# An eighth Strassen pair in the down projections, with their casts tied in order

## The chip, the cores and the metric

The kernel runs on one core of one Trainium2 chip. The metric is the device time of one execution in microseconds (us); lower is better. Three executions of the kernel before took 2194.71, 2195.12 and 2196.28 us, with the median 2195.12.

## The reference, cut to what matters

The program is one layer of a streaming encoder on 256 tokens of width 2048: a SwiGLU feed-forward block (FFN), gated token mixers, cross-attention, and a second FFN, each between two RMSNorms. The change touches the two FFNs alone:

```python
def swiglu(h, w_gate, w_up, w_down):
    return (jax.nn.silu(h @ w_gate) * (h @ w_up)) @ w_down
...
    h = rmsnorm(x, n_ffn1_pre[l])
    x = x + 0.5 * rmsnorm(swiglu(h, w_ffn1_gate[l], w_ffn1_up[l], w_ffn1_down[l]), n_ffn1_post[l])
```

`w_gate` and `w_up` are 2048 x 5504, `w_down` is 5504 x 2048, all f32. The down projection therefore sums over 5504 = 43 x 128 hidden units, that is over 43 k-tiles, which the kernel numbers k = 0 to 42.

## The kernel before

**Three matmuls for one.** The weights are f32. Each tile of weights `raw` is cut into a high part (`hi`, ScalarE cast to fp32r) and the rest (`lo = raw - hi`, VectorE subtraction). The activations are cut the same way, for the down projection into `mh` and `ml`. One product is then three TensorE matmuls: `mh*hi`, `mh*lo` and `ml*hi` (`product`, lines 544 to 546, in the wide part; lines 460 to 462 in `lin_tok_steps`, the narrow part).

**The down projection.** The 2048 output columns are done in two halves, b = 0 and b = 1, of 1024 columns; each half has two narrow columns, c = 2b and c = 2b + 1, of 512. The tokens are two groups t of 128. So a half has four accumulators `own[t][h]`, each one PSUM bank of 128 x 512. With four more banks (`shared`, called p1, p5, p7 and p6) all eight banks are in use.

**The wide part** (`lin_wide`) takes k = 0 to 29 with weight tiles of 128 x 1024. An ordinary k-tile takes 2 x 2 products, 12 matmuls, into `own`. The k-tiles 4 to 17 are taken as seven pairs (`SPAIRS`), with the Strassen-Winograd scheme: a pair would take eight products, and takes seven (21 matmuls). The sums of weights that this needs are four VectorE additions (lines 570 to 573) on the two raw tiles `ra` and `rb`, in place, after their own parts are cut. The sums of activations are made earlier, where gate and up end, by `left` (lines 510 to 513), and are kept in the tile `S`. Three products of a pair go straight to `own`, four to `shared`.

**Order.** `_wide_order` lists three ordinary k-tiles, then each pair followed by two ordinary ones. TensorE follows this order by hand (`manual_schedule`). On the other engines a list scheduler orders the instructions by priority when the program is built; `ahead(self.lead)` gives casts, splits and additions of weights a priority 100 steps earlier. `after(ins, prev)` adds an edge that fixes the order of two instructions. `cut` does a cast and a split; its outputs go round a ring of six slots, three of `whi`/`wlo` and three of `room`. In the first pair the cuts are, in order of the program: three ordinary tiles, the first half of `ra`, `rb`; then, after the additions, `ra` again and `rb` again; then the next two ordinary tiles. The first five are tied in this order by `after`, the later ones are not. The loads go round four `wraw` buffers and the two halves of a tile `raws`.

**After the wide part** comes `narrow(c + 1, 30 to 35)`, which continues the odd column's banks; then `fix_wide` adds the shared products onto the four banks of `own` (one ScalarE copy, line 594, and eight VectorE additions, lines 595 to 602, in a buffer `part` of the pool `wraw`); then `narrow(c, 30 to 42)` continues the even column's banks, `own[0][0]` and `own[1][0]`, and so waits for what `fix_wide` adds to them; then `narrow(c + 1, 36 to 42)`. In `narrow` one weight tile holds two k-tiles of 512 columns, and takes 2 x 2 x 3 = 12 matmuls. Its casts and splits are lines 365 and 366.

In the second half, `done` and `refill` start four loads of the residual X from POOL, two during the last pairs and two in `narrow(c + 1)`, because X has the memory that the first part of `S` had.

Of the kernel before, what the change touches and what calls it, by code (L numbers as in the profile page):

```python
# [10 lines left out]
F32 = mybir.dt.float32  # L11
# [7 lines left out]
P = 128  # L19
# [7 lines left out]
WT = 1024  # L27
# [6 lines left out]
LEAD = 100  # L34
FIRST = 1000000
TOK_US, CH_US = 0.65, 0.33
SPAIRS = range(2, 9)
WIDE, EARLY = 30, 36


def _wide_order():
# [184 lines left out]
class Layer:  # L226
# [275 lines left out]
            for t in range(NT):  # L502
                evac(t, ps[t])

    def left(self, g0, g1, mh, ml, k, sh, sl):


        nc = self.nc
        d = self.tmp.tile([P, 512], F32, tag="junk", name="sums").rearrange("p (a t) -> p a t", a=4)
        nc.vector.tensor_sub(d[:, 0], g0[:, P:], g1[:, P:])  # L510
        nc.vector.tensor_sub(d[:, 1], d[:, 0], g0[:, :P])
        nc.vector.tensor_sub(d[:, 2], g0[:, :P], g0[:, P:])
        nc.vector.tensor_add(d[:, 3], g1[:, :P], d[:, 1])
        self.split(g1, mh[:, k + 1, :], ml[:, k + 1, :])
        self.split(d[:, 0], mh[:, k, P:], ml[:, k, P:])
        self.split(d[:, 1:], sh, sl)

    def lin_wide(self, w, b, mh, ml, sums, ring, raws, banks, done):

        nc = self.nc
        own, shared = banks
        seen, turn = set(), [0]
        last = _wide_order()[-1]

        def cut(raw):
            n = raw.shape[-1]
            hi, lo = (x[:, :n] for x in ring[turn[0] % len(ring)])
            turn[0] += 1  # L530
            before = self.last_cast, self.last_split
            with self.ahead(self.lead):
                self.last_cast = nc.scalar.copy(out=hi, in_=raw)  # L533
                self.last_split = nc.vector.tensor_sub(out=lo, in0=raw, in1=hi.bitcast(F32))  # L534
            if turn[0] < 6:
                for ins, prev in zip((self.last_cast, self.last_split), before):
                    self.after(ins, prev)
            return [(self.paired(hi[:, i : i + 512]), self.paired(lo[:, i : i + 512])) for i in range(0, n, 512)]

        def product(bank, x, wt, stop=False):  # L540
            (xh, xl), (hi, lo) = x, wt
            start = id(bank) not in seen
            seen.add(id(bank))
            nc.tensor.matmul(bank, xh, hi, start=start, stop=False)  # L544
            nc.tensor.matmul(bank, xh, lo, start=False, stop=False)  # L545
            nc.tensor.matmul(bank, xl, hi, start=False, stop=stop)  # L546

        def load():
            i = self.wide_at % 6
            raw = raws[:, i - 4] if i > 3 else self.wraw.tile([P, WT], F32, tag="wraw", name="wraw")  # L550
            o = P * WT * (b * KF + self.wide_at)
            nc.sync.dma_start(out=raw, in_=w[o : o + P * WT].rearrange("(p x) -> p x", p=P))
            self.wide_at += 1
            return raw

        at = lambda k, t: tuple(x[:, k, t * P : (t + 1) * P] for x in (mh, ml))
        self.wide_at = 0
        for item in _wide_order():
            if isinstance(item, int):
                halves = cut(load())  # L560
                for t in range(NT):
                    for h in range(2):
                        product(own[t][h], at(item, t), halves[h], item == last)
                continue
            k0, k1 = item
            ra, rb = load(), load()
            a0, a1, b0, b1 = ra[:, :512], ra[:, 512:], rb[:, :512], rb[:, 512:]
            (w11,), (w21, w22) = cut(a0), cut(rb)
            with self.ahead(self.lead):
                nc.vector.tensor_add(a0, a0, a1)  # L570
                nc.vector.tensor_add(a1, a1, b1)  # L571
                nc.vector.tensor_add(b1, a0, b1)
                nc.vector.tensor_add(b0, b1, b0)
            (e1, e3), (e4, e2) = cut(ra), cut(rb)
            s2, s3, s4 = sums(k0 // 2 - SPAIRS[0])
            end = k0 // 2 == SPAIRS[-1]
            product(shared[0], at(k0, 0), w11, end)
            product(own[0][0], at(k1, 0), w21)
            product(own[0][1], s4, w22)
            product(shared[1], at(k0, 1), e1, end)  # L580
            product(shared[2], s3, e3, end)
            product(shared[3], s2, e2, end)
            product(own[1][0], at(k1, 1), e4)
            done(k0 // 2 - SPAIRS[0])
        self.cuts = turn[0]

    def fix_wide(self, banks, part):


        nc = self.nc  # L590
        own, (p1, p5, p7, p6) = banks
        u, v = part[:, :512], part[:, 512:]
        add, sub = nc.vector.tensor_add, nc.vector.tensor_sub
        self.after(nc.scalar.copy(out=u, in_=p1), self.last_cast)
        self.after(add(own[0][0], own[0][0], u), self.last_split)
        add(u, p6, u)
        sub(v, p5, u)
        add(u, p7, u)
        add(own[1][0], own[1][0], u)
        add(own[0][1], own[0][1], v)  # L600
        sub(v, v, p7)
        add(own[1][1], own[1][1], v)

    def rstd(self, ss, n, half=False, weight=1.0):

# [192 lines left out]
    def ffn(self, normed, wg, wu, wd, post, residual, *after):  # L798
# [3 lines left out]
        with self.tc.tile_pool(name="hid", bufs=1) as hid:  # L802
# [3 lines left out]
                 self.hpool.tile([P, 8, 2, P], F32R, tag="yh", bufs=2, name="S"))  # L806

            def sums(n):
                x, n = (S[0], n) if n < 5 else (S[1], n - 5)
                return x[:, 3 * n : 3 * n + 3]  # L810

            def evacs(c0):
                gate = {}

                def ev_gate(j, ps):
                    sg = hid.tile([P, T], F32, tag="sg", name="sg", bufs=2)
                    nc.vector.tensor_mul(sg, ps, row())
                    nc.scalar.activation(out=sg, in_=sg, func=AF.Silu)
                    nc.vector.tensor_mul(sg, sg, row())
                    gate[j] = sg  # L820

                def ev_up(j, ps):
                    k = c0 // P + j
                    nc.vector.tensor_mul(gate[j], ps, gate[j])
                    if k // 2 not in SPAIRS:
                        self.split(gate[j], mh[:, k, :], ml[:, k, :])
                    elif j == 0:
                        self.split(gate[j][:, :P], mh[:, k, :P], ml[:, k, :P])
                    else:
                        v = sums(k // 2 - SPAIRS[0])  # L830
                        self.left(gate[0], gate[1], mh, ml, k - 1, v[:, :, 0], v[:, :, 1])

                return ev_gate, ev_up

# [45 lines left out]
            def refill():  # L880
                i = fresh.pop()
                t, s = i // 2, slice(i % 2 * 1024, (i % 2 + 1) * 1024)
                self.after(nc.gpsimd.dma_start(
                    out=self.X[:, t, s], in_=residual[t * P : (t + 1) * P, s]), self.last_split)
# [11 lines left out]
            def lin(c, ev, passage):  # L896
                b = c // 2
                if c % 2:
                    narrow(c, range(EARLY, KF, 2), ev, (7 if passage else SKEW) * (c == 3), passage)
                    return  # L900
                make = lambda pool, tag: [pool.tile([P, 512], F32, tag=tag, name="mm") for _ in range(2)]
                one = [make(self.pst, "tr"), make(self.pss, "sm")]
                two = [make(self.psm, "mm"), make(self.psm, "mm")]
                own, shared = (two, one) if b else (one, two)
                banks[b] = [list(x) for x in zip(*own)], [x for p in shared for x in p]
                with self.tc.manual_schedule(engines={mybir.EngineType.PE}):
                    if b:
                        self.X = self.hpool.tile([P, NT, D], F32, tag="big", bufs=1, name="X")
                        fresh.extend((3, 2, 1, 0))
                    order = slots[self.turn :] + slots[: self.turn]  # L910
                    self.lin_wide(wd, b, mh, ml, lambda n: [(x[:, 0], x[:, 1]) for x in (sums(n)[:, i] for i in range(3))],
                                  order + more, raws, banks[b], lambda n: n > 4 and fresh and refill())
                    self.turn = (self.turn + self.cuts % (2 * RING)) % RING if self.cuts % (2 * RING) < RING else self.turn
                    narrow(c + 1, range(WIDE, EARLY, 2), None, 0, None)
                    self.fix_wide(banks[b], self.wraw.tile([P, WT], F32, tag="wraw", name="part"))
                    narrow(c, range(WIDE, KF, 2), ev, 0, None)

            return self.post_norm(lin, post, True, *after)
# [1024 lines left out]
```

## Time and profile before

| What | Value |
|---|---|
| median of three executions | 2195.12 us (2194.71 to 2196.28) |
| profiled execution | 2195.21 us |
| span from first to last instruction | 2193.4 us |
| TensorE (PE) busy, matmul | 2161.4 us, 99% |
| weight loads (PEld) | 1926.9 us, 88% |
| VectorE (DVE) | 1617.8 us, 74% |
| ScalarE (ACT) | 1190.3 us, 54% |
| HBM read | 438.61 MB |

The rows of the profile name an engine, a line of the kernel, the operation, the tiles written and read, and times in us (`xN` is a count; ns where said). "Idle before" an instruction is the time in which its engine waited, with the engine that ended the wait. A matmul's row is longer than the time until the next matmul may start, because matmuls overlap: TensorE's pace is read from starts.

### The profile page before, as it was taken

How to read it: one execution, taken by the hardware profiler on the slowest of the kernel's cores; microseconds unless marked ns; L12 is line 12 of the kernel's file. 1: busy time of each engine (PE TensorE's matmuls, PEld its weight loads, DVE VectorE, ACT ScalarE, POOL GpSimd, SP SyncE). 2: the span in 40 equal slices, each digit the busy share in tenths (PEclk: the TensorE clock that was granted, in tenths of full speed). 3: DMA queues.
4: the chain of work that ended last, by engine and by line, in shares of the span. 5: the costliest groups of instructions: out<-in, count | busy, mean ns of one | idle time of the engine just before them, and what ended most of it. 6: DMA issues, size and time to landing. Idle time of an engine off the chain costs nothing.

```text
span 2193.4 us, 35347 instructions
## 1 busy us (share of the span) xinstructions
PE 2161.4 (99%) x13580; PEld 1926.9 (88%) x13580; DVE 1617.8 (74%) x2402; ACT 1190.3 (54%) x1794; POOL 110.5 (5%) x185
## 2 busy tenths in 40 slices
PE   9999999999999999999999999999999999999998
PEld 8999999988888888988777889988999999998886
DVE  7777666688887677768778766657777766679696
ACT  7555555555556565664444556446555555555553
POOL 0000000000000000101342000000000000000000
PEclk9999999999999999999999999999999999999999
DMA  7666666665766664555867765546666666666665
GB/s 251 203 201 202 202 201 202 201 232 203 228 219 227 220 204 150 186 172 184 253 200 243 274 212 192 176 164 219 198 202 201 201 201 202 201 221 223 200 233 170
DMA packets 132361, 453.51 MB, mean 207 GB/s; under 512 B 16352, under 2 KB 17888, under 8 KB 131936
## 3 DMA queue, kind: packets, MB, share of 16 engines
q1 hardware_dynamic: 123408, 429.84, 59.4%
q0 software_dynamic: 7920, 20.98, 3.1%
q8 instruction: 106, 1.74, 0.3%
q10 hardware_dynamic: 864, 0.44, 0.1%
q14 instruction: 63, 0.52, 0.1%
HBM read 438.61 MB, written 12.59 MB: 206 GB/s over the span
## 4 chain that ended last, share of the span: by engine, by line
PE 45%; DVE 5%; issue 1%; DMA 1%; ACT 1%; POOL 0%; DVEq 0%; POOLq 0%; ACTq 0%
PE mm L421 16%; PE mm L425 8%; PE mm L460 5%; PE mm L462 4%; PE mm L461 4%; PE mm L545 2%; PE mm L546 2%; PE mm L544 2%; DVE wlo L366 2%; ACT whi L365 0%; DVE tm L1415 0%; DVE TT L1418 0%; PE xo L1817 0%; PE tr L663 0%; DMA raws<-in_w_ffn_down 0%
## 5 line engine op out<-in xcount | busy, mean ns | idle before, releaser
L366 DVE TENSOR_TENSOR wlo<-wraw,whi 128x1024 fp32r<-128x1024 f32 (+3 forms) x672 | 806.3, 1202 | 422.8 <-ACT whi L365 414.2
L421 PE MATMUL mm<-hT,whi 128*128 128x512 f32 x3280 | 1078.6, 384 | 0.7 <-DVE hT L654 0.7
L365 ACT CAST whi<-wraw 128x1024 fp32r<-128x1024 f32 (+3 forms) x672 | 692.0, 1031 | 580.8 <-PE mm L462 207.6
L425 PE MATMUL mm<-hT,wlo 128*128 128x256 f32 x3280 | 880.0, 274 | 0.6 <-DVE wlo L366 0.6
L421 PEld LDWEIGHTS mm<-hT,whi 128*128 128x128 f32 x3280 | 614.1, 190 | 81.7 <-ACT whi L365 1.2
L425 PEld LDWEIGHTS mm<-hT,wlo 128*128 128x128 f32 x3280 | 630.1, 192 | 6.7 <-DVE wlo L366 1.0
L461 PE MATMUL mm<-wlo,hT 128*128 128x512 f32 (+2 forms) x512 | 180.0, 352 | 4.0 <-DVE wlo L366 3.8
L460 PE MATMUL mm<-whi,hT 128*128 128x512 f32 (+2 forms) x512 | 182.5, 356 | 0.9 <-DVE gt L1602 0.7
L462 PE MATMUL mm<-whi,hT 128*128 128x512 f32 (+2 forms) x512 | 178.3, 349 | 0.3 <-DVE hT L654 0.3
L433 ACT COPY half<-mm 128x256 f32<-128x256 f32 x206 | 75.5, 368 | 115.6 <-PE mm L421 115.6
L434 DVE TENSOR_TENSOR half<-half,mm 128x256 f32<-128x256 f32 x206 | 85.7, 417 | 40.4 <-ACT half L433 40.4
L461 PEld LDWEIGHTS mm<-wlo,hT 128*128 128x128 f32 x512 | 97.1, 190 | 18.3 <-DVE wlo L366 9.5
L460 PEld LDWEIGHTS mm<-whi,hT 128*128 128x128 f32 x512 | 97.1, 190 | 12.6 <-DVE gt L1602 1.1
L544 PE MATMUL mm<-whi,mh 128*128 128x512 f32 x284 | 107.6, 379 | 0.0
L545 PE MATMUL mm<-wlo,mh 128*128 128x512 f32 x284 | 107.6, 379 | 0.0
L546 PE MATMUL mm<-whi,ml 128*128 128x512 f32 x284 | 107.6, 379 | 0.0
L462 PEld LDWEIGHTS mm<-whi,hT 128*128 128x128 f32 x512 | 97.1, 190 | 10.0 <-DVE hT L654 1.2
L534 DVE TENSOR_TENSOR wlo<-wraw,whi 128x1024 fp32r<-128x1024 f32 x60 | 72.0, 1222 | 18.3 <-ACT whi L533 17.7
L533 ACT CAST whi<-wraw 128x1024 fp32r<-128x1024 f32 x60 | 61.3, 1048 | 31.6 <-ACT whi L533 9.0
L533 ACT CAST room<-wraw 128x1024 fp32r<-128x1024 f32 (+1 forms) x56 | 49.6, 893 | 51.3 <-DVE wraw L571 46.4
L460 PE MATMUL mm<-whi,mh 128*128 128x512 f32 x200 | 75.8, 379 | 0.0
L461 PE MATMUL mm<-wlo,mh 128*128 128x512 f32 x200 | 75.8, 379 | 0.0
(373 smaller groups left out, 2787.8 us busy)
## 6 DMA issues: line engine op xcount, KB each, us to landing
wraw<-in_w_ffn_up SPq DMA_DIRECT2D x171, 512.0 KB, 4.3
wraw<-in_w_ffn_gate SPq DMA_DIRECT2D x170, 512.0 KB, 4.3
wraw<-in_w_ffn_down SPq DMA_DIRECT2D x128, 512.0 KB, 4.6
wraw<-in_w_in SPq DMA_DIRECT2D x124, 512.0 KB, 3.8
raws<-in_w_ffn_down SPq DMA_DIRECT2D x40, 512.0 KB, 4.9
wraw<-in_w_o SPq DMA_DIRECT2D x32, 512.0 KB, 4.3
wraw<-in_w_ckv SPq DMA_DIRECT2D x32, 512.0 KB, 4.1
wraw<-in_w_oa SPq DMA_DIRECT2D x16, 512.0 KB, 3.6
```

Source lines behind the costliest of these rows:

```text
L365: cast = self.last_cast = nc.scalar.copy(out=hi[:, e], in_=raw[:, e])
L366: self.last_split = nc.vector.tensor_sub(out=lo[:, e], in0=raw[:, e], in1=hi[:, e].bitcast(F32))
L421: both = lambda: nc.tensor.matmul(ps[j], hi[:, s], self.woven(x[:, k]), start=(k == 0), stop=(k == nk - 1))
L425: nc.tensor.matmul(ps[j][:, 0, :], lo[:, s], self.woven(x[:, k, 0]), start=False, stop=False)
L434: nc.vector.tensor_add(tokens, tokens, high)
L460: nc.tensor.matmul(ps[t], part(xh, t, k), hi, start=(k == first and not begun), stop=False, **more)
L461: nc.tensor.matmul(ps[t], part(xh, t, k), lo, start=False, stop=False, **more)
L462: self.last_mm = nc.tensor.matmul(ps[t], part(xl, t, k), hi, start=False, stop=(k == last), **more)
L533: self.last_cast = nc.scalar.copy(out=hi, in_=raw)
L544: nc.tensor.matmul(bank, xh, hi, start=start, stop=False)
L545: nc.tensor.matmul(bank, xh, lo, start=False, stop=False)
L546: nc.tensor.matmul(bank, xl, hi, start=False, stop=stop)
```

## The change

`SPAIRS` gets an eighth pair, k = 18 and 19, and the wide part grows from k < 30 to k < 34, so that each pair still has two ordinary k-tiles behind it. `narrow(c + 1)` before `fix_wide` shrinks from k = 30 to 35 to k = 34 and 35, and `narrow(c)` starts at 34. All cuts of the wide part are tied in order, not the first five alone. `fix_wide` works in `raws`, which the wide part no longer needs then, in place of a buffer of `wraw`; its additions start with `p6 + u`, and are tied one after another. The sums of activations of the first pair (n = 0) lie in what was left free in `S`, one block in its first tile and two in its second, so that `left` splits them in two instructions. The refill of X starts one pair later, with the two last pairs as before.

```diff
-SPAIRS = range(2, 9)
-WIDE, EARLY = 30, 36
+SPAIRS = range(2, 10)
+WIDE, EARLY = 34, 36
...
-    def left(self, g0, g1, mh, ml, k, sh, sl):
+    def left(self, g0, g1, mh, ml, k, places):
...
-        self.split(d[:, 1:], sh, sl)
+        i = 1
+        for x in places:
+            n = x.shape[1]
+            self.split(d[:, i : i + n], x[:, :, 0], x[:, :, 1])
+            i += n
...
-            if turn[0] < 6:
-                for ins, prev in zip((self.last_cast, self.last_split), before):
-                    self.after(ins, prev)
+            for ins, prev in zip((self.last_cast, self.last_split), before):
+                self.after(ins, prev)
...
-        u, v = part[:, :512], part[:, 512:]
+        (u, x), (v, z) = [(part[:, i, :512], part[:, i, 512:]) for i in range(2)]
         add, sub = nc.vector.tensor_add, nc.vector.tensor_sub
         self.after(nc.scalar.copy(out=u, in_=p1), self.last_cast)
-        self.after(add(own[0][0], own[0][0], u), self.last_split)
-        add(u, p6, u)
-        sub(v, p5, u)
-        add(u, p7, u)
-        add(own[1][0], own[1][0], u)
-        add(own[0][1], own[0][1], v)
-        sub(v, v, p7)
-        add(own[1][1], own[1][1], v)
+        prev = self.last_split
+        for f, *args in ((add, x, p6, u), (sub, v, p5, x), (add, x, p7, x), (add, own[0][0], own[0][0], u),
+                         (add, own[1][0], own[1][0], x), (sub, z, v, p7), (add, own[0][1], own[0][1], v),
+                         (add, own[1][1], own[1][1], z)):
+            ins = f(*args)
+            self.after(ins, prev)
+            prev = ins
...
             def sums(n):
-                x, n = (S[0], n) if n < 5 else (S[1], n - 5)
-                return x[:, 3 * n : 3 * n + 3]
+                if n == 0:
+                    return S[0][:, 15:], S[1][:, 6:]
+                x, n = (S[0], n - 1) if n < 6 else (S[1], n - 6)
+                return (x[:, 3 * n : 3 * n + 3],)
...
-                                  order + more, raws, banks[b], lambda n: n > 4 and fresh and refill())
+                    self.lin_wide(wd, b, mh, ml, parts, order + more, raws, banks[b],
+                                  lambda n: n > 5 and fresh and refill())
...
                     narrow(c + 1, range(WIDE, EARLY, 2), None, 0, None)
-                    self.fix_wide(banks[b], self.wraw.tile([P, WT], F32, tag="wraw", name="part"))
+                    self.fix_wide(banks[b], raws)
                     narrow(c, range(WIDE, KF, 2), ev, 0, None)
```

More of the change, by code (lines that the diff above doesn't have):

```diff
@@ L808, in sums, with parts @@
             def sums(n):
-                x, n = (S[0], n) if n < 5 else (S[1], n - 5)
-                return x[:, 3 * n : 3 * n + 3]
+                if n == 0:
+                    return S[0][:, 15:], S[1][:, 6:]
+                x, n = (S[0], n - 1) if n < 6 else (S[1], n - 6)
+                return (x[:, 3 * n : 3 * n + 3],)
+            def parts(n):
+                return [(x[:, i, 0], x[:, i, 1]) for x in sums(n) for i in range(x.shape[1])]
             def evacs(c0):
@@ L829, in ev_up @@
                     else:
-                        v = sums(k // 2 - SPAIRS[0])
-                        self.left(gate[0], gate[1], mh, ml, k - 1, v[:, :, 0], v[:, :, 1])
+                        self.left(gate[0], gate[1], mh, ml, k - 1, sums(k // 2 - SPAIRS[0]))
                 return ev_gate, ev_up
@@ L910, in lin @@
                     order = slots[self.turn :] + slots[: self.turn]
-                    self.lin_wide(wd, b, mh, ml, lambda n: [(x[:, 0], x[:, 1]) for x in (sums(n)[:, i] for i in range(3))],
-                                  order + more, raws, banks[b], lambda n: n > 4 and fresh and refill())
+                    self.lin_wide(wd, b, mh, ml, parts, order + more, raws, banks[b],
+                                  lambda n: n > 5 and fresh and refill())
                     self.turn = (self.turn + self.cuts % (2 * RING)) % RING if self.cuts % (2 * RING) < RING else self.turn
                     narrow(c + 1, range(WIDE, EARLY, 2), None, 0, None)
-                    self.fix_wide(banks[b], self.wraw.tile([P, WT], F32, tag="wraw", name="part"))
+                    self.fix_wide(banks[b], raws)
                     narrow(c, range(WIDE, KF, 2), ev, 0, None)
```

## The prediction

> **What bounds the kernel now.** I read the page first, then the busy time of two windows, the waits of TensorE, and last the instructions in order of time around the start and the end of the wide part. From the page:
>
> ```profile
> span 2193.4 us, 35347 instructions
> PE 2161.4 (99%) x13580; PEld 1926.9 (88%) x13580; DVE 1617.8 (74%) x2402; ACT 1190.3 (54%) x1794; POOL 110.5 (5%) x185
> L544 PE MATMUL mm<-whi,mh 128*128 128x512 f32 x284 | 107.6, 379 | 0.0
> ```
>
> TensorE is the bound, so the change is worth the matmuls it takes away and the time in which TensorE waits. For the price of a matmul the 379 ns of its row won't do, as rows overlap. The first matmul of the narrow part behind the wide one, and the one 36 matmuls later (k = 30 to 35, six each):
>
> ```profile
> 534.33 0.38 PE L460 MATMUL mm<-whi,mh 128*128 128x512 f32 x1
> 542.10 0.38 PE L460 MATMUL mm<-whi,mh 128*128 128x512 f32 x1
> ```
>
> 7.77 us for 36 matmuls is 0.216 us each. That is the price here.
>
> The windows (length, then busy time of PE, PEld, DVE, ACT and POOL, each with its count, clock, DMA share, GB/s), one in the gate and up stage, one in the middle of a wide part:
>
> ```profile
> 60.00:440.00 380.00, 380.00 (x2323) 349.43 (x2322) 270.93 (x405) 201.18 (x305) 0.00 (x0) 1.00 0.62 201
> 480.00:527.00 47.00, 47.00 (x220) 41.15 (x219) 44.62 (x51) 27.18 (x29) 0.00 (x0) 1.00 0.64 217
> ```
>
> In both TensorE has no gap. But in the wide part VectorE is at 44.62 of 47.00, 95%, against 71% in gate and up: the wide part has little room on VectorE, and a late start there shows. It does, in the waits of TensorE:
>
> ```profile
> PE mm L545 <- DVE wlo L534: 3.5, 4, 1.0
> ```
>
> Four waits, one in each wide part (two FFNs, two halves), for a split of the wide part. The row counts from the modelled end of the matmul before, so the loss is read from starts. These are the matmuls, in order, around each such wait: first and third matmul of the product e1 of the first pair (line 544 `room,mh`, 546 `room,ml`), then of its product e2 (`whi,S`); in the first wide part e1 has no gap.
>
> ```profile
> 470.86 0.38 PE L544 MATMUL mm<-whi,S 128*128 128x512 f32 x1
> 472.60 0.38 PE L546 MATMUL mm<-whi,S 128*128 128x512 f32 x1
> ...
> 577.71 0.38 PE L544 MATMUL mm<-room,mh 128*128 128x512 f32 x1
> 578.45 0.38 PE L546 MATMUL mm<-room,ml 128*128 128x512 f32 x1
> 579.32 0.38 PE L544 MATMUL mm<-whi,S 128*128 128x512 f32 x1
> 580.73 0.38 PE L546 MATMUL mm<-whi,S 128*128 128x512 f32 x1
> ...
> 1975.29 0.38 PE L544 MATMUL mm<-room,mh 128*128 128x512 f32 x1
> 1976.18 0.38 PE L546 MATMUL mm<-room,ml 128*128 128x512 f32 x1
> 1977.04 0.38 PE L544 MATMUL mm<-whi,S 128*128 128x512 f32 x1
> 1978.78 0.38 PE L546 MATMUL mm<-whi,S 128*128 128x512 f32 x1
> ...
> 2083.89 0.38 PE L544 MATMUL mm<-room,mh 128*128 128x512 f32 x1
> 2084.64 0.38 PE L546 MATMUL mm<-room,ml 128*128 128x512 f32 x1
> 2085.50 0.38 PE L544 MATMUL mm<-whi,S 128*128 128x512 f32 x1
> 2086.91 0.38 PE L546 MATMUL mm<-whi,S 128*128 128x512 f32 x1
> ```
>
> Two steps of 0.216 would be 0.43 us. What is over: at e2 1.31, 0.98, 1.31 and 0.98, at e1 0.31, 0.46 and 0.32; in all 5.67 us.
>
> Why the splits are late is in VectorE's and ScalarE's instructions of the first of these places:
>
> ```profile
> 465.13 0.69 DVE L571 TENSOR_TENSOR wraw<-wraw,raws 128x512 f32<-128x512 f32 x1
> ...
> 466.06 0.68 DVE L572 TENSOR_TENSOR raws<-wraw,raws 128x512 f32<-128x512 f32 x1
> 466.67 1.22 DVE L534 TENSOR_TENSOR wlo<-raws,whi 128x1024 fp32r<-128x1024 f32 x1
> 467.80 0.68 DVE L573 TENSOR_TENSOR raws<-raws 128x512 f32<-128x512 f32 x1
> 468.41 1.22 DVE L534 TENSOR_TENSOR room<-wraw,room 128x1024 fp32r<-128x1024 f32 x1
> ...
> 469.88 1.22 DVE L534 TENSOR_TENSOR wlo<-wraw,whi 128x1024 fp32r<-128x1024 f32 x1
> 471.01 1.22 DVE L534 TENSOR_TENSOR wlo<-raws,whi 128x1024 fp32r<-128x1024 f32 x1
> 466.16 1.04 ACT L533 CAST room<-wraw 128x1024 fp32r<-128x1024 f32 x1
> 468.81 1.03 ACT L533 CAST whi<-raws 128x1024 fp32r<-128x1024 f32 x1
> ```
>
> By the ring of six slots, the split at 466.67 is the ordinary tile behind the pair, and that at 469.88 the second one. TensorE needs both after the pair. The pair's own splits, at 468.41 (for e1 and e3) and 471.01 (for e2), stand behind them; the last ends at 472.23, and TensorE goes on at once.
>
> **The change, part by part.**
>
> *Matmuls.* A pair takes 21 matmuls in place of 24. One more pair in each of four wide parts: 4 x 3 x 0.216 = 2.59 us less on the path. The four k-tiles that pass from narrow to wide have 12 matmuls per half either way. The Trainium skill, in "TensorE: Matmul & The Clock Gate", section Back-to-back issue gap, gives about 131 ns as the sustained step of LDWEIGHTS and matmul pairs at N = 512, and 216 ns for the isolated gap; by the former this part would be 12 x 0.131 = 1.57 us and the time 2188.0. The 7.77 us for 36 such pairs are at the latter.
>
> *The tie.* With every cut tied, the casts and splits at 466.67 and 469.88 go behind the pair's. L573 starts at 466.67, 1.13 us earlier; ScalarE casts `ra` when L571 is done (465.82, cast until 466.9) and `rb` when L573 is (467.4, until 468.5); VectorE's two splits then end at about 468.5 and 469.7. That is 2.2 to 2.5 us before 472.23. The waits were 0.98 to 1.31 us at e2, with e1's in front at most 1.77 (1.31 + 0.46, third place), so each goes, with 0.4 us over in the tightest. Gain 5.67 us. The bounds: nothing, if something else holds the split, and 5.67, since no more is there; I take 5.67, as both splits in front are seen. What is late next: the first ordinary tile, split by about 470.9; without the wait TensorE comes to its low part seven matmuls after 470.86, at 472.4. Then the second pair: VectorE has the same work up to there, TensorE comes 1.3 us earlier. VectorE gains about 0.5 us on it per pair (5% of 45 x 0.216 = 9.7 us). No new wait.
>
> *Junction.* Where the wide part ends, the cover of `fix_wide` shrinks, from 36 matmuls (7.77 us) to 12 (2.59 us):
>
> ```profile
> 528.54 1.23 DVE L366 TENSOR_TENSOR wlo<-wraw,whi 128x1024 fp32r<-128x1024 f32 x1 [0.42 <-ACT whi L365]
> 533.02 1.23 DVE L366 TENSOR_TENSOR wlo<-wraw,whi 128x1024 fp32r<-128x1024 f32 x1 [3.25 <-ACT whi L365]
> 535.61 1.23 DVE L366 TENSOR_TENSOR wlo<-wraw,whi 128x1024 fp32r<-128x1024 f32 x1 [1.37 <-ACT whi L365]
> 536.75 0.69 DVE L595 TENSOR_TENSOR mm<-mm,part 128x512 f32<-128x512 f32 x1
> ...
> 539.65 0.70 DVE L599 TENSOR_TENSOR mm<-mm,part 128x512 f32<-128x512 f32 x1
> 530.88 0.38 PE L546 MATMUL mm<-whi,S 128*128 128x512 f32 x1
> 535.48 0.58 ACT L594 COPY part<-mm 128x512 f32<-128x512 f32 x1
> ```
>
> Five additions, 0.725 us apart, lead to the two banks that `narrow(c)` needs; before they start at 536.75 because they are tied behind the third narrow split (535.61). After, `narrow(c + 1)` has one load, so they and the copy are tied behind the first (528.54). The last matmul that they wait for is p6's, at 530.88, so they can start at 531.3; own[1][0] also needs the ordinary tile, done before 534.33. Five additions end at 534.9, or 536.1 with the split of 533.02 between them (1.14 more). TensorE comes to own[0][0] at 534.33 + 2.59 = 536.92, to own[1][0] 0.65 later. So 0, with about 1 us over; without this cover it is the second rival. Bounds: 0, and 2.7 us each (below). Zero is nearer, since the tie to 535.61 is gone.
>
> *Raw tile.* `raws` in place of `part` leaves one `wraw` buffer to the loads. TensorE had no gap behind the junction, so 0. The 44 loads per half on SP's queue stay 44.
>
> *Left.* One pair more per FFN in gate and up: four additions
>
> ```profile
> L513 DVE TENSOR_TENSOR sums<-sg,sums x14: 280/284/289, 77.4 to 1708.9; 128x128 f32<-128x128 f32 x14
> ```
>
> of 0.28 us, and three more splits (the first pair's in two included), each under the 1.22 us of a 1024-wide one: at most 4.8 us on VectorE, in a stage where it idles 380 - 271 = 109 us and TensorE never. 0. Without that cover it would be up to 4.8 per FFN.
>
> *Refill.* Two of POOL's four loads of X start one pair later, with 75 narrow matmuls (16.2 us) still ahead of X's first use: 0.
>
> *Sum.* 2195.21 (profiled execution; 2193.4 of span and 1.8 around it) - 2.59 - 5.67 = 2186.95, so 2187.0. The profiled execution stands 0.09 above the median, less than the runs differ.
>
> **The rivals.**
>
> *The tie frees nothing.* If e2 still waits (something else puts the split there, or ScalarE's strict order delays the casts), only the matmuls are left: 2192.6. Against it: the rows show two splits, 2.27 us, ahead of the one that was 1.31 late. If half of the waits go: 2189.8.
>
> *The junction opens* (slower). If the scheduler places the additions behind the two narrow splits, as now at 536.75, own[0][0], fourth in the new order, is ready at 536.75 + 3 x 0.725 + 0.69 = 539.6, while TensorE needs it at 536.92: 2.7 us at each of four places, 10.8, and 2197.8. One more split ahead (1.14 each) gives 2202.3. It decides from 8.26 / 4 = 2.07 us per place, that is where own[0][0] is ready later than 539.0. For it: priorities put splits of weights ahead of the additions. Against: these splits wait for slots that TensorE frees later than p6.
>
> *VectorE becomes the bound of the wide part* (slower). The eighth pair and its two tiles bring 0.95 x 9.7 = 9.2 us to VectorE and take four narrow splits (4 x 1.13) away: 4.7 us per half; all of it on the path would be 18.8 - 8.3 = 10.5 us more, 2205.7. It decides where VectorE's share passes 100%; the window has 95%. The Trainium skill, in "VectorE: DVE Perf Modes", section Rules for kernel authors, advises few instructions rather than fused ones, which speaks against more pairs. The trace agrees with a fixed cost: 0.68 us for 512 columns, 1.22 for 1024.
>
> **How the numbers follow.** Forecast 0.66 (2185.5 to 2188.5 by itself); half or none of the waits gone 0.19; junction 0.10; VectorE 0.02; 0.03 for reordering elsewhere, either way. 0.2% is 4.4 us, about what a measurement tells from no change: faster means below 2190.7, slower above 2199.5. Faster: the forecast, half of the second case, some of small openings of the junction: 0.77. Same: 2192.6 and 2197.8: 0.17. Slower: a junction with one more split, or VectorE: 0.06. The range goes from 2185.2 to 2192.8: it holds the forecast and the case of matmuls alone, and leaves the junction out.
>
> **What would show it.** Look for 12 fewer 512-wide matmuls in lines 460 to 462 and 544 to 546 together, steps of 0.43 us from line 544 to 546 in every first pair, the pair's two splits directly behind L573, additions of `fix_wide` beginning within 1 us of p6's last matmul, and no gap at the first matmul of `narrow(c)`. A wait of line 460 for the additions, or a wait of line 545 in later pairs, would make the prediction wrong.

## The result, and the profile after

| | before | after |
|---|---|---|
| median, this chip | 2195.45 us (2193.34 to 2196.28, 6 executions) | 2186.85 us (2184.9 to 2189.39, 6 executions) |
| ratio | | 0.996 [0.995, 0.9971] |
| profiled execution | 2195.21 us | 2186.96 us |
| its span | 2193.4 us | 2185.0 us |

The kernel is faster by 8.6 us by the medians. The prediction was 2187.0. In the kernel after, the lines of the wide part are 3 to 4 higher: the cast is line 537, the split 538, the three matmuls 547 to 549, the four additions 573 to 576, and all additions of `fix_wide` are line 602.

Two lines of the page of the kernel after, span and engines:

```profile
span 2185.0 us, 35393 instructions
PE 2157.1 (99%) x13568; PEld 1924.8 (88%) x13568; DVE 1636.9 (75%) x2440; ACT 1195.2 (55%) x1808; POOL 110.9 (5%) x185
```

13568 matmuls against 13580: the 12 fewer that four more pairs give, at a total of busy time 4.3 us lower. VectorE does more (19.1 us), and TensorE does not feel it. The same two windows as before:

```profile
60.00:440.00 380.00, 380.00 (x2323) 349.47 (x2322) 272.26 (x412) 202.09 (x308) 0.00 (x0) 1.00 0.62 201
480.00:527.00 47.00, 47.00 (x219) 41.15 (x219) 46.11 (x51) 27.71 (x31) 0.00 (x0) 1.00 0.67 230
```

In gate and up nothing has changed for TensorE, though VectorE has 1.3 us more to do there. In the wide part VectorE's share went from 95% to 98%, and TensorE still has no gap.

The largest waits of TensorE in the kernel after (us in total, times, longest) have no row for a split of the wide part any more:

```profile
PE mm L461 <- DVE wlo L366: 3.9, 7, 1.4
PE tr L665 <- ACT hn L976: 1.8, 3, 0.9
```

Where the time went is read from the starts of the four wide parts and of the stage behind the first FFN. Before:

```profile
459.83 0.38 PE L544 MATMUL mm<-whi,mh 128*128 128x512 f32 x1
568.00 0.38 PE L544 MATMUL mm<-whi,mh 128*128 128x512 f32 x1
674.27 0.33 PE L168 MATMUL tr<-ident,X 128*128 128x128 f32 x1
1965.57 0.38 PE L544 MATMUL mm<-whi,mh 128*128 128x512 f32 x1
2074.18 0.38 PE L544 MATMUL mm<-whi,mh 128*128 128x512 f32 x1
```

and after:

```profile
460.19 0.38 PE L547 MATMUL mm<-whi,mh 128*128 128x512 f32 x1
566.38 0.38 PE L547 MATMUL mm<-whi,mh 128*128 128x512 f32 x1
670.72 0.33 PE L168 MATMUL tr<-ident,X 128*128 128x128 f32 x1
1962.01 0.38 PE L547 MATMUL mm<-whi,mh 128*128 128x512 f32 x1
2068.20 0.38 PE L547 MATMUL mm<-whi,mh 128*128 128x512 f32 x1
```

| From, to | before | after | difference | three matmuls + waits of this first pair |
|---|---|---|---|---|
| FFN 1, first half | 108.17 | 106.19 | -1.98 | 0.65 + 1.31 = 1.96 |
| FFN 1, second half | 106.27 | 104.34 | -1.93 | 0.65 + 0.98 + 0.31 = 1.94 |
| end of FFN 1 to start of wide part in FFN 2 | 1291.30 | 1291.29 | -0.01 | 0 |
| FFN 2, first half | 108.61 | 106.19 | -2.42 | 0.65 + 1.31 + 0.46 = 2.42 |
| FFN 2, second half, to the start of its last matmul | 107.91 | 105.97 | -1.94 | 0.65 + 0.98 + 0.32 = 1.95 |
| from there to the end of the span | 11.34 | 10.87 | -0.47 | 0 |

All four halves come out within 0.02 us. The last matmul of the kernel starts at 2182.09 before and at 2174.18 after; behind it another 0.47 us are gone, which no term of the prediction covers. They go with the new `fix_wide`: this stretch takes 11.33 us in `tie_only`, which has the old one, and 10.87 in `fix_only`, which has the new one. Why is not shown. The first wide part starts 0.36 us later than before. In the profiles of all 13 kernels of this document it starts between 459.39 and 461.00, so such a difference needs no cause in the change.

### The profile page after: what moved, and what is told of

The parts are those of the page before. It is cut to its first block, busy times and chain, and to the rows that moved or that the text cites. A ratio compares the mean times of both kernels' runs of the same rounds, so it can differ in the third digit from the quotient of the medians.

```text
span 2185.0 us, 35393 instructions
## 1 busy us (share of the span) xinstructions
PE 2157.1 (99%) x13568; PEld 1924.8 (88%) x13568; DVE 1636.9 (75%) x2440; ACT 1195.2 (55%) x1808; POOL 110.9 (5%) x185
## 4 chain that ended last, share of the span: by engine, by line
PE 88%; DVE 6%; ACT 2%; issue 2%; DMA 1%; POOL 0%; DVEq 0%; ACTq 0%; POOLq 0%
PE mm L421 32%; PE mm L425 16%; PE mm L460 7%; PE mm L462 7%; PE mm L461 7%; PE mm L548 5%; PE mm L549 5%; PE mm L547 5%; DVE wlo L366 2%; ACT whi L365 1%; DVE tm L1421 0%; PE tr L665 0%; PE xo L1823 0%; DVE TT L1424 0%; DVE X L771 0%
## 5 line engine op out<-in xcount | busy, mean ns | idle before, releaser
L366 DVE TENSOR_TENSOR wlo<-wraw,whi 128x1024 fp32r<-128x1024 f32 (+3 forms) x656 | 787.2, 1202 | 391.2 <-ACT whi L365 383.2
L365 ACT CAST whi<-wraw 128x1024 fp32r<-128x1024 f32 (+3 forms) x656 | 674.7, 1030 | 552.4 <-PE mm L462 195.7
L547 PE MATMUL mm<-whi,mh 128*128 128x512 f32 x320 | 121.3, 379 | 0.0
L548 PE MATMUL mm<-wlo,mh 128*128 128x512 f32 x320 | 121.3, 379 | 0.0
L549 PE MATMUL mm<-whi,ml 128*128 128x512 f32 x320 | 121.3, 379 | 0.0
L537 ACT CAST room<-wraw 128x1024 fp32r<-128x1024 f32 (+1 forms) x68 | 60.3, 895 | 73.9 <-DVE wraw L574 70.8
L538 DVE TENSOR_TENSOR wlo<-wraw,whi 128x1024 fp32r<-128x1024 f32 x72 | 86.0, 1222 | 16.4 <-ACT whi L537 15.1
L537 ACT CAST whi<-wraw 128x1024 fp32r<-128x1024 f32 x72 | 73.0, 1046 | 29.8 <-PE mm L462 8.7
L538 DVE TENSOR_TENSOR room<-wraw,room 128x1024 fp32r<-128x1024 f32 (+1 forms) x68 | 69.7, 1029 | 0.0
L549 PEld LDWEIGHTS mm<-whi,ml 128*128 128x128 f32 x320 | 60.5, 189 | 8.6
```

The costliest lines, as they stand in the source:

```text
L365: cast = self.last_cast = nc.scalar.copy(out=hi[:, e], in_=raw[:, e])
L366: self.last_split = nc.vector.tensor_sub(out=lo[:, e], in0=raw[:, e], in1=hi[:, e].bitcast(F32))
```

## The experiments

### The tie without the eighth pair

`tie_only` is the kernel before with every cut of the wide part tied:

```diff
-            if turn[0] < 6:
-                for ins, prev in zip((self.last_cast, self.last_split), before):
-                    self.after(ins, prev)
+            for ins, prev in zip((self.last_cast, self.last_split), before):
+                self.after(ins, prev)
```

> The kernel before with one edit: every cut of the wide part is tied to the one before it; seven pairs, the old order and buffer of the additions in PSUM stay. Theory (the waits at e1 and e2 of the first pair come from the two ordinary tiles' splits in front of the pair's own): all four waits go, 5.67 us, so about 2189.5 us (ratio 0.9974 to before), and no step over 0.5 us from the first to the third matmul of e1 or e2 in any first pair. Rival 1 (the tie frees nothing, the eighth pair brings the gain): 2195, ratio 1.000. Rival 2 (the tie and the junction work only together): in between, with a new wait at the narrow part.

Measured: 2189.91 us, ratio 0.9971 [0.9961, 0.9981], that is 6.4 us less (4.2 to 8.6). The row of waits for line 534 is gone, and in the wide parts no step between matmuls is longer than 0.22 us. Cut as in the table, the four halves are 1.33, 1.28, 1.77 and 1.29 us shorter than before, 5.67 in all. The tie alone takes the four waits away.

### The eighth pair without the tie

`pair_no_tie` is the kernel after with the tie again under the old condition:

```diff
-            for ins, prev in zip((self.last_cast, self.last_split), before):
-                self.after(ins, prev)
+            if turn[0] < 6:
+                for ins, prev in zip((self.last_cast, self.last_split), before):
+                    self.after(ins, prev)
```

> The changed kernel with the tie put back to the first five cuts; the eighth pair and the new additions stay. Theory: the matmuls alone, 12 x 0.216 = 2.59 us, so about 2192.8 us (ratio 0.9988 to before), with TensorE's waits for the split of line 538 back in all four first pairs, 1.0 to 1.8 us each. Rival 1 (the eighth pair brings the gain): 2187. Rival 2 (an eighth pair without the tie makes VectorE late in the later pairs too): over 2195, with waits in pairs after the first.

Measured: 2193.05 us, ratio 0.9986 [0.9977, 0.9995], 3.1 us less than before (1.1 to 5.0). Its waits of TensorE have the old row under its new line numbers:

```profile
PE mm L549 <- DVE wlo L538: 3.5, 4, 1.0
```

and VectorE has the old order: an ordinary split ahead of the fourth addition, and another ahead of the split for e2.

```profile
466.69 1.22 DVE L538 TENSOR_TENSOR wlo<-raws,whi 128x1024 fp32r<-128x1024 f32 x1
467.83 0.68 DVE L577 TENSOR_TENSOR raws<-raws 128x512 f32<-128x512 f32 x1
...
469.90 1.22 DVE L538 TENSOR_TENSOR wlo<-wraw,whi 128x1024 fp32r<-128x1024 f32 x1
471.04 1.22 DVE L538 TENSOR_TENSOR wlo<-raws,whi 128x1024 fp32r<-128x1024 f32 x1
```

Cut as in the table, its four halves are 0.41, 0.64, 0.96 and 0.65 us shorter than before, 2.66 in all. The two parts of the change are separate: 6.4 and 3.1 us alone, 8.6 together, with intervals of 2 us on each side of the first two.

### The tie in the first pair alone

`tie_first_pair` puts `if turn[0] < 10:` in place of `if turn[0] < 6:` in the edit just shown, so that only the first nine cuts are tied, those up to the two ordinary tiles behind the first pair.

> The changed kernel with the tie on the first nine cuts alone, that is up to the two ordinary tiles behind the first pair; the later cuts are untied. Theory (the tie's whole worth is the order in the first pair; before, the later pairs were in order without it): the same as the changed kernel, 2187 us, ratio 0.996 to before. Rival (the ties of the later cuts keep the scheduler from another bad order, with eight pairs): over 2189, with waits for a split of line 538 in a later pair.

Measured: 2186.99 us, ratio 0.996 [0.9947, 0.9972], as the kernel after. No wait for line 538 is left. All that the tie is worth lies in the first pair and its two ordinary tiles; the order of the later pairs comes out well enough by itself.

### The new `fix_wide` alone

`fix_only` is the kernel before with the new order of `fix_wide` and the buffer `raws`, and nothing else of the change (its additions tied one after another, p6 first).

> The kernel before with the additions in PSUM alone as changed: their new order, tied one after another, in the tile raws. Seven pairs, the old tie. Theory: nothing on TensorE's path, since before it had no gap behind the wide part: 2195.2, ratio 1.000 within 0.0015. Rival 1 (the buffer of wraw that is left to the loads was worth something): 2193 or less. Rival 2 (the chain of ties, or the wait for the last raws tile, delays the even column): over 2197, with a wait at the first matmul of the narrow part's second column.

Measured: 2195.43 us, ratio 0.9997 [0.9988, 1.0006]: nothing that shows within 2 us. Its trace has the waits of before at e1 and e2, and behind its last matmul the 0.47 us less of the table above.

### The junction without its cover

`no_cover` takes away the twelve matmuls of `narrow(c + 1)` that lie ahead of `narrow(c)`; they are done behind it:

```diff
-WIDE, EARLY = 34, 36
+WIDE, EARLY = 34, 34
```

> The changed kernel with EARLY = 34: no narrow k-tile of the odd column lies between the wide part and the even column; its two k-tiles, 34 and 35, pass to the end of the odd column. The same matmuls in all. Theory (12 matmuls, 2.59 us, cover the five additions, of which the first bank's end 0.9 us and the second's 1.5 us after the last wide matmul): without the cover TensorE waits about 1.0 us at the first matmul of the even column at each of four places, 4 us in all, about 2190.8 us. Rival 1 (the additions are early enough by themselves, the 12 matmuls cover nothing): 2187. Rival 2 (splits of the narrow part get in front of the additions, 2.7 us or more at each place): 2197 to 2202.

Measured: 2191.55 us, ratio 0.9979 [0.997, 0.9988], 4.7 us above the kernel after. The waits of TensorE name the additions, once at each of the four junctions, and the matmuls of the first junction show the size:

```profile
PE mm L460 <- DVE mm L602: 3.6, 4, 0.9
```

```profile
543.74 0.38 PE L549 MATMUL mm<-whi,ml 128*128 128x512 f32 x1
545.02 0.46 PE L460 MATMUL mm<-whi,mh 128*128 128x512 f32 x1 [0.90 <-DVE mm L602]
545.31 0.38 PE L461 MATMUL mm<-wlo,mh 128*128 128x512 f32 x1
```

From the last matmul of the wide part to the first of `narrow(c)` there are 1.28 us and then 0.29, in place of 0.216 each: 1.14 us lost at each junction, 4.5 us over the four. The rival of the opening junction is a real mechanism, and the twelve matmuls left in front are what keeps it shut.

### A longer chain in `fix_wide`

Four more VectorE instructions that change no value stand ahead of the addition into `own[0][0]` (`fix_longer`); `fix_longer2` has two:

```diff
+        same = lambda o, p, q: nc.vector.tensor_tensor(out=o, in0=p, in1=q, op=ALU.max)
...
-        for f, *args in ((add, x, p6, u), (sub, v, p5, x), (add, x, p7, x), (add, own[0][0], own[0][0], u),
+        for f, *args in ((add, x, p6, u), (sub, v, p5, x), (add, x, p7, x), (same, x, x, x), (same, x, x, x), (same, x, x, x), (same, x, x, x),
+                         (add, own[0][0], own[0][0], u),
```

> The changed kernel with four more 128x512 VectorE instructions (maximum of a tile with itself, no value changes) in the chain of additions in PSUM, ahead of the addition to own[0][0]: 2.6 to 2.9 us more before the even column's first bank is ready. Theory (it is ready 1.7 us before TensorE comes, 543.98 against 545.66 in the first wide part): TensorE waits 1.0 to 2.3 us at the first matmul of the even column, and up to 1.1 again for own[1][0], at each of four places; 4 to 13 us in all, 2191 to 2200. The lower end if the additions stay together, the upper if two narrow splits get between them. Rival 1 (the cover is not what holds it, the additions have far more room): 2187. Rival 2 (no cover at all): four times 2.7 and more, with waits also where the odd column begins.

Measured: 2208.6 us, ratio 1.0058 [1.0045, 1.0072], over the range of the theory. The four first waits are 2.1, 2.1, 2.1 and 2.7 us long, where 1.0 to 2.3 were expected, and no matmul waits for the additions where the odd column begins, as it would have by the second rival. What follows the waits was not foreseen. TensorE in `fix_longer`, at the first junction:

```profile
544.72 0.38 PE L462 MATMUL mm<-whi,ml 128*128 128x512 f32 x1
547.20 0.76 PE L460 MATMUL mm<-whi,mh 128*128 128x512 f32 x1 [2.10 <-DVE mm L604]
547.75 0.63 PE L461 MATMUL mm<-wlo,mh 128*128 128x512 f32 x1
548.18 0.63 PE L462 MATMUL mm<-whi,ml 128*128 128x512 f32 x1
...
549.43 0.63 PE L461 MATMUL mm<-wlo,mh 128*128 128x512 f32 x1
549.86 0.63 PE L462 MATMUL mm<-whi,ml 128*128 128x512 f32 x1
...
550.67 0.38 PE L461 MATMUL mm<-wlo,mh 128*128 128x512 f32 x1
550.89 0.38 PE L462 MATMUL mm<-whi,ml 128*128 128x512 f32 x1
```

The first step is 2.48 us in place of 0.216, a loss of 2.26. Then the matmuls start 0.43 us apart, half the rate, until 550.67, and only there 0.22 again: the seven steps from 547.20 take 3.47 us in place of 1.51 (part of that is the second wait, for `own[1][0]`, at 548.84). In the row of this stretch among the windows the granted clock, the column behind POOL's busy time, is down:

```profile
544.50:552.00 7.50, 5.37 (x17) 3.70 (x16) 6.05 (x9) 1.09 (x2) 0.00 (x0) 0.77 0.59 205
```

The four junctions lose 4.22, 5.05, 4.89 and 5.61 us, 19.8 in all. The medians of this kernel and the kernel after are 21.8 us apart, the profiled spans 18.8. With two added instructions in place of four:

> The changed kernel with two more 128x512 instructions in the chain of additions in PSUM, where fix_longer has four. In fix_longer TensorE waited 2.1 to 2.7 us for own[0][0] and 0.8 for own[1][0], and then ran eight matmuls at 0.43 us in place of 0.216, with a granted clock of 0.77 in that stretch. Theory 1 (1.4 us less in the chain; one narrow split less in front): waits of 0 to 0.9 us per place, no matmul at 0.43 behind them, a granted clock of 1.00, and 2187 to 2191. Theory 2 (the slow matmuls come with any wait at this place): the granted clock falls in these stretches too, and 2194 or more.

Measured: 2191.12 us, ratio 0.998 [0.9971, 0.999]. At three junctions 0.94 + 0.07 us are lost, at the fourth 1.62 + 0.07, together 4.7, against 4.3 us between the medians; up to 0.9 was expected at a place. No matmul behind these waits runs at half rate. Its row for the same stretch:

```profile
544.50:552.00 7.50, 6.72 (x32) 5.60 (x31) 6.93 (x9) 2.71 (x3) 0.00 (x0) 1.00 0.71 246
```

The clock stays at 1.00, here and at the other three junctions. At the first junction the two instructions and one more narrow split stand ahead of the addition into `own[0][0]`, 1.33 + 1.13 = 2.46 us more against the room of 1.7 us, which leaves 0.8 us of the 0.94 lost there. So the room is real, a longer chain costs what goes beyond it, and `fix_longer` paid once more for the clock.

### One more VectorE instruction in each pair

This is the test of the rival in which VectorE becomes the bound. `dve_more` adds one instruction per pair (`dve_more2` two) behind the four additions; it changes no value:

```diff
+                nc.vector.tensor_tensor(out=b0, in0=b0, in1=b0, op=ALU.max)
```

> The changed kernel with one more VectorE instruction per pair behind the four additions, a 128x512 maximum of a tile with itself, which changes no value (0.66 us of start to start). Theory (VectorE takes 9.24 us per pair and its two ordinary tiles, by the starts of line 576 from 467.31 to 513.52, TensorE 45 x 0.216 = 9.72): 9.90, so VectorE loses 0.2 us per pair on TensorE, 1.3 to 1.5 by the eighth; about 1 us of lead in the first pair takes most of that, so 0 to 1 us per half, 2187 to 2191. Rival 1 (VectorE bounds the wide part already): 32 x 0.66 = 21 us, 2208. Rival 2 (VectorE is far from bounding it): 2187, with no new wait, and the same for two such instructions.

> The same with two such instructions per pair. Theory: VectorE takes 10.6 us per pair, 0.85 more than TensorE; over seven periods 6 us per half, less 1 us of lead: 4 x 5 = 20 us and some 0.1 us after each wait, so about 2207 to 2210, with waits for splits of line 538 in every pair from the second or third on. Rival 1 (VectorE bounds the wide part already): 42 us, 2229. Rival 2 (VectorE is far from bounding): 2187.

Measured: 2227.23 us, ratio 1.0144 [1.013, 1.0158], and 2254.98 us, 1.0272 [1.0257, 1.0288]. One instruction of 0.69 us costs 40 us over 32 pairs, 1.26 each: twice its own time on VectorE, and far over every expectation. Yet VectorE is not full in `dve_more`; it is busy less than in the kernel after:

```profile
480.00:527.00 47.00, 43.12 (x191) 35.37 (x190) 40.65 (x47) 24.59 (x27) 0.00 (x0) 1.00 0.56 191
```

40.65 of 47.00 is 86%. VectorE in `dve_more` in one pair, then ScalarE in the pair before and in this one:

```profile
499.82 0.69 DVE L576 TENSOR_TENSOR raws<-raws 128x512 f32<-128x512 f32 x1
500.43 1.22 DVE L538 TENSOR_TENSOR room<-wraw,room 128x1024 fp32r<-128x1024 f32 x1
501.56 0.68 DVE L577 TENSOR_TENSOR raws<-raws 128x512 f32<-128x512 f32 x1
503.43 2.36 DVE L538 TENSOR_TENSOR wlo<-raws,whi 128x1024 fp32r<-128x1024 f32 x2 [1.19 <-ACT whi L537]
```

```profile
491.42 2.94 ACT L537 CAST whi<-wraw 128x1024 fp32r<-128x1024 f32 x3 [2.14 <-DVE wraw L577]
...
502.36 1.99 ACT L537 CAST whi<-raws 128x1024 fp32r<-128x1024 f32 x2 [2.14 <-PE mm L549]
```

The added instruction (line 577) lands behind the split of `ra`, and ScalarE can cast `rb` only when it is done, at 502.24. In the pair before, the row of the cast names line 577; here a matmul ended within 0.02 us of line 577 and is named in its place. VectorE's next instruction by the ties is the split of `rb`, which needs that cast: so VectorE stands for 1.19 us with work in its queue that it may not do. From one line 577 to the next there are 10.94 us (490.62 to 501.56), against 45 x 0.216 = 9.7 us of matmuls for the pair and its two ordinary tiles. TensorE waits 32 times:

```profile
PE mm L548 <- DVE wlo L538: 24.3, 32, 0.8
```

and from the second pair on the steps around that wait are 1.22 us too long; over all four wide parts the steps are 38.0 us too long. With two instructions TensorE waits for the cast as well (23.8 us in 32 waits). Two kernels tell the cause apart, the instruction's time or its place. In `dve_beside` an equal instruction reads the activations, writes a scratch tile, and stands behind the four additions with nothing behind it in the chain:

```diff
-                nc.vector.tensor_add(b0, b1, b0)
+                last_add = nc.vector.tensor_add(b0, b1, b0)
+                scratch = self.tmp.tile([P, 512], F32, tag="junk", name="beside")
+                some = mh[:, 0:2, :].rearrange("p a t -> p (a t)").bitcast(F32)
+                self.after(nc.vector.tensor_tensor(out=scratch, in0=some, in1=some, op=ALU.max), last_add)
```

> The changed kernel with one more 128x512 VectorE instruction per pair, as in dve_more, but off the pair's chain: it reads mh, writes a scratch tile, and is tied behind the last addition, so that no cast waits for it. Theory 1 (what made dve_more 40 us slower is the place in the chain, as the cast of rb waits for the instruction and VectorE then idles 1.19 us in each pair with nothing it may do in the strict order): VectorE takes 9.24 + 0.66 = 9.90 us per pair against TensorE's 9.72, so 0 to 1 us per half, 2187 to 2191, and no idle of VectorE before the split of rb. Theory 2 (VectorE has no room at all in the wide part, any instruction costs its whole length and more): 2208 to 2227.

Measured: 2187.84 us, ratio 0.9965 [0.995, 0.998]: as the kernel after. The window, and VectorE in one pair:

```profile
480.00:527.00 47.00, 47.00 (x220) 41.12 (x219) 46.48 (x55) 25.98 (x30) 0.00 (x0) 1.00 0.65 224
```

```profile
496.21 0.69 DVE L576 TENSOR_TENSOR raws<-raws 128x512 f32<-128x512 f32 x1
496.82 0.69 DVE L579 TENSOR_TENSOR beside<-mh 128x512 f32<-128x512 f32 x1
497.42 1.22 DVE L538 TENSOR_TENSOR room<-wraw,room 128x1024 fp32r<-128x1024 f32 x1
498.56 2.36 DVE L538 TENSOR_TENSOR wlo<-raws,whi 128x1024 fp32r<-128x1024 f32 x2
```

VectorE at 46.48 of 47.00, 99%, does not stop TensorE in the wide part: the cast of `rb` runs under the added instruction and the split of `ra`, and the split of `rb` waits for nothing. The four wide parts are as long as in the kernel after to 0.1 us. Behind them the second half of each FFN is longer in this profile, by 1.1 and 1.6 us, which no run explains. `dve_more_untied` is `dve_more` with the tie of `tie_first_pair`:

> dve_more (the extra instruction in the chain, ahead of the cast of rb) with the tie on the first nine cuts alone, so that the scheduler may put other work in front of rb's split from the second pair on. Theory 1 (the idle 1.19 us comes from the strict order, which leaves VectorE nothing to do while ScalarE casts rb): VectorE fills it, its period falls from 10.93 to about 9.9 us, and most of the 40 us go: 2188 to 2197. Theory 2 (the longer chain itself is the limit, with any order): 2220 or more.

Measured: 2194.76 us, ratio 0.9997 [0.9987, 1.0006]. Of the 40 us 32 are gone. Its waits of TensorE for these splits are 8, in the first two pairs of each wide part:

```profile
PE mm L549 <- DVE wlo L538: 6.4, 8, 1.2
```

So most of the 40 us came from the place in the chain under a strict order, not from VectorE's load. The 8 us that are left lie in the first pair, which is tied, and in the second, which is not tied and still loses 0.9 us each time.

## Why the prediction was right, point by point

**Matmuls, -2.59.** 12 fewer stand in the page. Alone (`pair_no_tie`) they gave 3.1 us [1.1 to 5.0] by the medians and 2.66 by the starts, and each half of the table above has its 0.65 us. The price of 0.216 us held. By the 131 ns of the Trainium skill ("TensorE: Matmul & The Clock Gate", Back-to-back issue gap) a half would, by an estimate from that figure, have won 0.39 us by its matmuls, and all four halves close within 0.02 us with 0.65: the trace does not agree with that figure.

**Tie, -5.67.** Alone (`tie_only`) it gave 6.4 us [4.2 to 8.6] by the medians and 5.67 by the starts. In the kernel after the two splits stand where the prediction put them, directly behind the last addition but for a short split of activations (line 653). VectorE in the first pair, then TensorE at its e2:

```profile
467.31 0.69 DVE L576 TENSOR_TENSOR raws<-raws 128x512 f32<-128x512 f32 x1
467.92 1.22 DVE L538 TENSOR_TENSOR room<-wraw,room 128x1024 fp32r<-128x1024 f32 x1
469.05 0.42 DVE L653 TENSOR_TENSOR ml<-sg,mh 128x256 fp32r<-128x256 f32 x1
469.39 2.35 DVE L538 TENSOR_TENSOR wlo<-raws,whi 128x1024 fp32r<-128x1024 f32 x2
```

```profile
471.20 0.38 PE L547 MATMUL mm<-whi,S 128*128 128x512 f32 x1
471.63 0.38 PE L549 MATMUL mm<-whi,S 128*128 128x512 f32 x1
```

The split for e2 is the first of two in the last VectorE row (1.22 each, 1.13 apart), done at about 470.6: 1.6 us earlier than the 472.23 of before, not 2.5. The prediction had the order of the splits but not the 0.36 us by which the whole half starts later, nor the instruction of line 653 (0.34 us); these are 0.7 of the 0.9 us. It was enough: e2's three matmuls go at steps of 0.43 us for two, the first at 471.20.

**Junction, 0.** The additions start 0.5 us after p6's last matmul, as the prediction asked. VectorE, then TensorE (p6's last matmul, first of `narrow(c)`), at the first junction of the kernel after:

```profile
540.10 2.14 DVE L602 TENSOR_TENSOR raws<-mm,raws 128x512 f32<-128x512 f32 x3 [1.60 <-PE mm L549]
542.16 1.21 DVE L366 TENSOR_TENSOR wlo<-wraw,whi 128x1024 fp32r<-128x1024 f32 x1
543.29 1.29 DVE L602 TENSOR_TENSOR mm<-mm,raws 128x512 f32<-128x512 f32 x2
```

```profile
539.62 0.38 PE L549 MATMUL mm<-whi,S 128*128 128x512 f32 x1
...
545.66 0.38 PE L460 MATMUL mm<-whi,mh 128*128 128x512 f32 x1
```

Three additions, then one narrow split (the case that the prediction counted with 1.14 us), then the two that `narrow(c)` needs. `own[0][0]` is ready at 543.29 + 0.69 = 543.98, and TensorE comes to it at 545.66: 1.7 us of room, where the prediction had about 1: it set the end of the fifth addition, 536.1, against the time for the bank of the fourth, 536.92. `no_cover` shows what stood behind it: 2.59 us of cover less, and 1.14 us lost per junction, as 2.59 - 1.7 = 0.9 says to within 0.25 us.

**Raw tile, left, refill, 0.** `fix_only` shows no cost of the raw tile or the new order. The gate and up window has no gap. The stretch from the end of FFN 1 to the next wide part is the same to 0.01 us, but that is luck: over the 13 profiles it takes 1289.7 to 1295.4 us.

**VectorE.** This rival was rightly given little, but its point of decision was incomplete. The prediction said that it decides where VectorE's share passes 100%. No run has a share over 100% with the added work beside the chain. `dve_beside` is at 99% without loss in the wide part and `dve_more` loses 40 us at 86%: below 100% what decides is whether an instruction stands between an addition and a cast that the next split in the tied order waits for.

**Luck in the number.** The sum was 8.26 us, and the two profiled executions differ by 8.25. The mechanism holds half by half, but agreement this close is in part luck: the 0.47 us gained behind the last matmul, which the prediction did not have, and the 0.36 us lost ahead of the first wide part nearly cancel, and six executions of the kernel after spread over 4.5 us.

**Left open.** Why the new `fix_wide` shortens the stretch behind the last matmul by 0.47 us.

## What to carry to other kernels

A list scheduler that puts ordinary work ahead of work needed sooner is cheap to correct by ties, and the profile shows the place: count the instructions of the late engine between the input being ready and the output. But a tied order turns each cross-engine step inside it into a possible stand of the whole engine, so tie only where the wait is (here the first pair, which gave all of it), and put extra work where a cast or a copy of another engine runs beside it. Judge an engine by what stands in its chain before a wait, not by its share of busy time.

## What the runs showed of the hardware

In `fix_longer` TensorE ran at about half rate behind each junction, 0.43 us from start to start in place of 0.216, with a granted clock of 0.77 to 0.82 in windows of 7.5 to 9.5 us around it. At the first junction this began right behind a wait of 2.1 us and lasted seven steps. At the other three the matmuls behind the first wait (2.1, 2.1 and 2.7 us) still went at 0.216, and the half rate came only behind a second wait of 0.76 us, which ended 1.6 us after the first. The slow stretches cost 1.7 to 2 us beyond the waits. After waits of 0.8 to 1.5 us (`no_cover`, `fix_longer2`, and 32 times in `dve_more`) the clock stayed at 1.00. Whether the length of one wait or the sum of two decides, and where the bound lies, no run here shows.
